# Gate and up products with the tokens stationary and 512 weight columns moving

## The chip, the cores and the metric

One core of a Trainium2 chip runs the whole program. The metric is the device time of one execution in microseconds (us). Before the change the median of 3 runs is 1294.36 us (1293.99 to 1295.44).

In what follows TensorE (PE) multiplies matrices: a *stationary* 128x128 operand is loaded first (PEld), then the columns of a *moving* operand stream through it and the result adds up in a PSUM bank of 128x512 float32. VectorE (DVE), ScalarE (ACT) and GpSimd (POOL) do the elementwise work, SyncE's queue (SP) issues the loads.

## The reference

One decoder layer on 256 tokens of width 2048: four recurrent mixers, an output product, and then the part that the change touches:

```
n = rmsnorm(x, ffn_norm)                                   # x: 256 x 2048
x = x + (silu(n @ w_gate) * (n @ w_up)) @ w_down           # w_gate, w_up: 2048 x 5632, w_down: 5632 x 2048
return rmsnorm(x, final_norm)
```

All inputs and the output are float32.

## The kernel before

**Products in three parts.** A float32 operand is split into a high part (rounded to the float32r format) and a low part (the rest). A product is high x high + high x low + low x high, that is three matmuls: the helper `mm3` (lines 167 to 172) issues them from lines 169, 170 and 171.

**Weights.** All weights lie in DRAM as blocks of 128 x 1024 float32 (512 KB) in the order of use, listed by `plan` (lines 45 to 55). `weights` (line 149) traces the load of a block on SP's queue (`raw`, 4 buffers), the rounding on ACT (`whi`, 3 buffers) and the subtraction on DVE (`wlo`, 3 buffers); it traces them with a raised priority (`PRIO` = 20), so that a planner, which orders each engine's instructions by priority and readiness, puts them ahead of about 20 instructions traced before them.

**Stages.** The mixers run first, between products with `w_in`. Then `w_out` (line 1183) adds the output product to x, and by `transpose_in` (line 361) transposes the new x on TensorE: two k tiles go through one bank, ACT writes the high part into `nhi[128, 16, 256]` (hidden position on the partitions, k tile, token), DVE the low part into `nlo`. The last four k tiles are made by `first()` inside the first gate product.

**Gate and up before (`ffn`, line 1240, with `group`, line 374).** 22 steps, each with 256 hidden channels of gate and 256 of up. A block of weights is 4 k tiles x 256 columns, so a product takes 4 blocks. The weights are the stationary side (128 channels), the 256 tokens of `nhi` or `nlo` the moving side:

```
a = (bank[:, h * T : h * T + T], w[0][:, kk, hs], w[1][:, kk, hs], *acts[k])
```

This is 16 k tiles x 2 channel halves x 3 = 96 matmuls of 256 columns per product, 4224 in all. The result lies with channels on the partitions, so the scale of a token (`rs1`, one number per token) must lie along the free dimension: `scales` (line 262) spreads it to a tile `R` with two small float32 matmuls. DVE multiplies the gate bank by `R` (line 1254), ACT takes the silu (line 1255), DVE multiplies the up bank by `R` (line 1256), and POOL multiplies both (line 1257) into the tiles `H`, which already have the layout that the down product needs.

**Down (`ffn`, lines 1273 to 1304).** Two passes over 44 k tiles with 1024 output columns each. Here `H`, split by `split` (line 1175), is the stationary side (128 tokens), and 512 weight columns are the moving side: 12 matmuls of 512 columns per block, 1056 in all, in four banks per pass. Between the passes DVE adds the four banks to x (`add`, line 1265). After the second pass come the last norm and the output.

**Banks.** After the mixers `bank` (line 115) hands out the 8 PSUM banks in a fixed rotation of their three pools (`big` with 3, `mx` with 4, `mxl` with 1 bank).

Of the kernel before, what the change touches and what calls it, by code (L numbers as in the profile page):

```python
# [9 lines left out]
AF = mybir.ActivationFunctionType  # L10
ALU = mybir.AluOpType
PSUM = bass.MemoryType.PSUM
P = 128
# [29 lines left out]


def plan():
    """the 128 x 1024 blocks that the weights are loaded in: (array, first row tile, row tiles, first column, columns)"""
    units = []
    cols = [RW + c for c in range(0, 1792, 256)] + [RG + c for c in range(0, 1024, 256)] + [o + c for o in (GD, ML) for c in range(0, 2048, 256)]
    for c in cols:
        units += [("w_in", k, 4, c, 256) for k in range(0, KT, 4)]  # L50
    units += [("w_out", k, 2, c, 512) for c in range(0, D, 512) for k in range(0, KT, 2)]
    for c in range(0, HID, 256):
        units += [(w, k, 4, c, 256) for w in ("ffn_w_gate", "ffn_w_up") for k in range(0, KT, 4)]
    units += [("ffn_w_down", k, 1, c, 1024) for c in range(0, D, 1024) for k in range(HT)]
    return units

# [2 lines left out]


def lay_out(inputs):
    """the inputs in the layouts that the kernel loads; nothing but reshapes, transposes, slices and concatenations"""
    import numpy as np

    A = {k: np.asarray(v) if k == "final_norm" else np.asarray(v)[0] for k, v in inputs.items()}
    r = {"x": A["x"], "final_norm": A["final_norm"]}
    r["xT"] = A["x"].T.reshape(KT, P, T).transpose(1, 0, 2)
    r["chan"] = np.concatenate([A[k].reshape(n, P) for k, n in CHAN]).T
    u = np.empty((len(UNIT_AT), P, UNIT), A["w_in"].dtype)
    for (w, k, nk, c, n), i in UNIT_AT.items():  # L70
        u[i] = A[w][k * P : (k + nk) * P, c : c + n].reshape(nk, P, n).transpose(1, 0, 2).reshape(P, UNIT)
    r["units"] = u
    g = np.concatenate([A["w_in"][:, o + 2048 : o + 2056] for o in (GD, ML)], axis=1)
    r["gate_w"] = g.reshape(KT, P, 16).transpose(1, 0, 2).reshape(P, 256)
    z = np.zeros(4, g.dtype)
    r["gate_b"] = np.stack([np.concatenate([A["gdn_dt_bias"], z, A["mlstm_b_i"], A["mlstm_b_f"]]), np.concatenate([A["gdn_a_log"], z, z, z])], axis=1)
    r["lora"] = np.concatenate([np.concatenate([A["rwkv_w2"], A["rwkv_a2"]]), A["rwkv_g2"]], axis=1)
    r["rglru"] = np.concatenate([A[k].transpose(1, 0, 2).reshape(P, 512) for k in ("rglru_w_a", "rglru_w_x")], axis=1)
    return {k: np.ascontiguousarray(v) for k, v in r.items()}


class Emitter:
# [30 lines left out]
        return self.pp.tile([P, 512], F32, name=self.nm("mxl"), tag="mxl", bufs=1)  # L113

    def bank(self):
        """a PSUM bank for the large products: from all of them once the mixers are done"""
        if self.gens or self.phase == 1:
            return self.big()
        self.nb += 1
        return (self.big, self.mx, self.big, self.mx, self.big, self.mx, self.mxl, self.mx)[self.nb % 8]()  # L120
# [4 lines left out]
        self.slot_of = {}  # L125

    def S(self, k=1, c="A"):
        """a [128, 512 k] tile in the rotating slots of lifetime class c"""
        key = c if k == 1 else "D"
        if not self.free_slots[key]:  # L130
            keys = [x for x in ("A", "B", "L", "D") if self.free_slots[x] and (k == 1 or x == "D")]
            if not keys:
                raise MemoryError(f"no slot for {key}")
            key = keys[0]
        q = self.free_slots[key]
        i = q.pop(0)
        w = 1024 if key == "D" else 512
        t = self.spool.tile([P, w], F32, name=self.nm(f"s{key}{i}"), tag=f"slot{key}{i}")
        if w != 512 * k:
            t = t[:, 0 : 512 * k]  # L140
        self.slot_of[id(t)] = (key, i, t)
        return t
# [29 lines left out]
        return i  # L172

    def behind(self):
        """PE instructions of the block stay behind the large products traced so far"""
        return self.tc.issue_after(self.last_mm.ins)

    def tick(self, k=1):
        """the mixers' next steps; HOLD has the ticks by which a step is late, to let its operands come"""
        self.acc += k  # L180
        while self.acc >= 1:
            self.acc -= 1
            for g in list(self.gens):
                name, gen, step, hold = g
                if hold:
                    g[3] -= 1
                    continue
                try:
                    next(gen)
                except StopIteration:  # L190
                    self.gens.remove(g)
                g[2] += 1
                g[3] = HOLD.get((name, g[2]), 0)
# [55 lines left out]
        return banks  # L249

    def squares(self, c):
        """sums of squares of x's columns 512c..512c+511; the last call gives the reciprocal roots"""
        nc = self.nc
        xs = self.S(2)
        nc.sync.dma_start(xs.rearrange("p (a n) -> p a n", a=2), self.A["x"].rearrange("(a p) d -> p a d", p=P)[:, :, c * 512 : c * 512 + 512])
        nc.scalar.activation(xs[:, 0:512], xs[:, 0:512], AF.Square, accum_out=self.ss[:, 0, c : c + 1])
        nc.vector.scalar_tensor_tensor(xs[:, 512:1024], xs[:, 512:1024], 1.0, xs[:, 512:1024], op0=ALU.mult, op1=ALU.mult, accum_out=self.ss[:, 1, c : c + 1])
        self.free(xs)
        if c == 3:
            self.rs0 = self.rstd(self.ss, "rs0")  # L260

    def scales(self, rs):
        """R: rs[token] on every partition"""
        nc = self.nc
        z = self.mx()
        for a in range(2):
# [13 lines left out]
        return i  # L280

    def normalise(self, u):
        """the normalised activations of k tiles 2u and 2u + 1, from the unnormalised parts"""
        nc = self.nc
        hi, lo = self.nhi[:, 2 * u : 2 * u + 2, :], self.nlo[:, 2 * u : 2 * u + 2, :]
        f = self.xt[u // 2].rearrange("p (k t) -> p k t", k=4)[:, 2 * (u % 2) : 2 * (u % 2) + 2, :]
# [85 lines left out]
                nc.vector.scalar_tensor_tensor(self.nlo[:, k, :], t[:, j * T : j * T + T], wcol[:, k : k + 1], self.nhi[:, k, :].bitcast(F32), op0=ALU.mult, op1=ALU.subtract)  # L372

    def group(self, name, col, tm=False, acts=None, pre=None):
        """products with 256 columns of a weight: two halves of a bank, by channel tile or (tm) by token tile"""
        bank = self.bank()
        acts = acts or [(self.nhi[:, k, :], self.nlo[:, k, :]) for k in range(KT)]
        first = None
# [20 lines left out]


class Lag:
    """TensorE instructions of the mixers, ordered behind the next few large products"""

    def __init__(self, em):
        self.em = em
# [8 lines left out]


def sums(em, mat, t, wait=0):
    """mat' t for a matrix of few bits, t in two parts"""
    nc = em.nc
    hi, lo = em.S(c="B"), em.S(c="B")
    h, l = hi.bitcast(F32R), lo.bitcast(F32R)  # L420
# [24 lines left out]


def evict(f):
    """the instructions that empty a bank of the large products go before those of the mixers"""

    def g(em, *a, **k):  # L450
        with em.tc.high_priority(offset=EPRIO):
# [36 lines left out]


def solve_blocks(em, q0, nq, steps, n=32):  # L490
    """inv <- (I - M)^-1 per partition; blk holds M transposed ([q, tau, t]), inv starts as the identity"""
    nc = em.nc
    blk, inv, tmp = em.blk[q0 : q0 + nq], em.inv[q0 : q0 + nq], em.tmp[q0 : q0 + nq]
    for j in range(n - 1):
# [24 lines left out]
def rwkv_half(em, hf, LX, R, K, V):  # L519
# [69 lines left out]
    sc = em.const([P, 2, 4], em.nm("sc"))  # L589
    nc.vector.tensor_tensor(sc[:, :, 0:3], E1.rearrange("p (a c t) -> p a c t", a=2, t=64)[:, :, 0:3, 63], em_.rearrange("p (a c) -> p a c", a=2)[:, :, 1:4], op=ALU.mult)  # L590
    em.free(E1, E2, E3, kk, a)
    # bonus
    for j in range(2):
        nc.vector.scalar_tensor_tensor(halves(t1)[j], halves(R)[j], PT["rwkv_r_k"][:, pr[j] : pr[j] + 1], halves(K)[j], op0=ALU.mult, op1=ALU.mult)
    em.free(R, K)
# [31 lines left out]
    def gmv(c, h, s):  # L627
        return GM[c // 2][:, (c % 2) * 512 + h * P + s * 64 : (c % 2) * 512 + h * P + s * 64 + 64]

    # token-major v and k,b  # L630
    VS, KT_ = em.S(2), em.S(2)
    nc.gpsimd.memset(VS[64:128, :], 0.0)
    for cc in range(2):
# [42 lines left out]
    nc.vector.tensor_copy(XT.rearrange("p (u n) -> p u n", n=64)[64:96, :, 32:64], zx[64:96, :].rearrange("p (u n) -> p u n", n=32))  # L676
    em.free(U)
    yield
    # chunk chain
    zy = em.mxl()  # L680
    sy = Seq(em)
    Y = None
# [83 lines left out]

@evict
def silu2(em, X, src=None):
    """X <- 2 silu(src)"""
    nc = em.nc  # L770
    src = X if src is None else src
    th = em.S()
# [20 lines left out]
def gates_mm(em):  # L793
# [41 lines left out]
    nc.scalar.activation(em.neg, GT[:, 1, 1, 0:4], AF.Exp, scale=-1.0)  # L835
    nc.vector.tensor_scalar(em.neg, em.neg, -1.0, None, op0=ALU.mult)
    yield
    # mLSTM: c = i - b, M = max(0, cummax c), exp(-m)
    em.c = em.const([P, 2, 4], "ccol")
    nc.vector.tensor_tensor(em.c, GT[:, 0, :, 8:12], GT[:, 1, :, 12:16], op=ALU.add)  # L840
    t = em.mx()
# [18 lines left out]


def bcast_rows(em, d, hf):
    """the rows 2hf and 2hf + 1 of d, on every partition"""
    z = em.S(c="B")
    em.nc.sync.dma_start(z, d[2 * hf : 2 * hf + 2].rearrange("h t -> (h t)").partition_broadcast(P))
    return z
# [292 lines left out]

@evict  # L1160
def gelu2(em, bank):
    """2 gelu(bank), tanh form; only needs the bank"""
    nc = em.nc
    g, t = em.S(), em.S()
    nc.scalar.activation(g, bank, AF.Copy, scale=0.5)
# [74 lines left out]
def ffn(em, first):  # L1240
    nc, A = em.nc, em.A
    H = []
    v2 = lambda t: t.rearrange("p (a b) -> p a b", a=2)
    for f in range(HID // 256):
        if f % 2 == 0:
            H.append(em.S(2))
        h = H[-1][:, (f % 2) * 512 : (f % 2) * 512 + 512]
        gb = em.group("ffn_w_gate", f * 256, pre=(lambda u: first() if u == 1 else None) if f == 0 else None)
        if f == 0:
            em.scales(em.rs1)  # L1250
        Rb = em.R[:, 0:T].unsqueeze(1).to_broadcast([P, 2, T])
        ub = em.group("ffn_w_up", f * 256)
        t, u = em.S(), em.S()
        nc.vector.tensor_tensor(v2(t), v2(gb), Rb, op=ALU.mult)
        nc.scalar.activation(t, t, AF.Silu)
        nc.vector.tensor_tensor(v2(u), v2(ub), Rb, op=ALU.mult)  # L1256
        nc.gpsimd.tensor_tensor(h, t, u, op=ALU.mult)  # L1257
        em.free(t, u)
    em.free(em.R)
    fn = [em.S() for _ in range(4)]  # L1260
    for n in range(4):
        nc.gpsimd.dma_start(fn[n], A["final_norm"][n * 512 : n * 512 + 512].partition_broadcast(P))
# [10 lines left out]
    for n in range(2):  # L1273
# [8 lines left out]
        for k in range(HT):  # L1282
            if k % 2 == 0:
                if hs and k <= HT - TAIL:
                    em.free(*hs)
                hs = split(em, H[k // 4][:, (k % 4) * T : (k % 4) * T + 512])
            whi, wlo = em.weights("ffn_w_down", k, 1, n * 1024, 1024)
            hi, lo = (t.bitcast(F32R) for t in hs)
            tail.append((k, hi, lo, whi, wlo))
            if n == 0 or k < HT - TAIL:  # L1290
# [146 lines left out]
```

## Time and profile before

| | |
|---|---|
| median of 3 runs | 1294.36 us |
| span of the profiled execution, first to last instruction | 1292.7 us |
| median less span | 1.66 us |
| PE busy | 97% of the span |
| DVE, ACT, POOL busy | 63%, 48%, 11% |
| granted TensorE clock, mean of the span | 0.991 |

The profile is of one execution and gives no time of it but the span; what lies before the first and after the last instruction is taken as the difference to the median. A line of the profile names engine, source line and operation, then `output<-input` by the program's names (`sA`, `sD` are the rotating SBUF slots, `big`, `mx`, `mxl` PSUM banks). Matmuls overlap, and a matmul's shown duration runs from its start to its modelled end. So what one of them costs in a stream is the distance from its start to the start of the next, not its duration.

### The profile page before, as it was taken

How to read it: one execution, taken by the hardware profiler on the slowest of the kernel's cores; microseconds unless marked ns; L12 is line 12 of the kernel's file. 1: busy time of each engine (PE TensorE's matmuls, PEld its weight loads, DVE VectorE, ACT ScalarE, POOL GpSimd, SP SyncE). 2: the span in 40 equal slices, each digit the busy share in tenths (PEclk: the TensorE clock that was granted, in tenths of full speed). 3: DMA queues.
4: the chain of work that ended last, by engine and by line, in shares of the span. 5: the costliest groups of instructions: out<-in, count | busy, mean ns of one | idle time of the engine just before them, and what ended most of it. 6: DMA issues, size and time to landing. Idle time of an engine off the chain costs nothing.

```text
span 1292.7 us, 22536 instructions
## 1 busy us (share of the span) xinstructions
PE 1259.0 (97%) x9244; PEld 1173.2 (91%) x9244; DVE 817.7 (63%) x1068; ACT 620.2 (48%) x809; POOL 142.4 (11%) x145
## 2 busy tenths in 40 slices
PE   9899999999899999999999999999999999999997
PEld 8789989988888888999999999999999988888885
DVE  6975799665698765755555555555555555557554
ACT  7664784436543544643333334333344444445443
POOL 1520210213401120000000000000100000001000
PEclk9999999999899999999999999999999999999999
DMA  8554436344544455555555555555655655555553
GB/s 328 184 161 125 139 117 184 129 151 131 166 160 134 136 170 194 171 183 183 180 180 185 189 181 180 180 191 185 201 194 177 193 184 194 195 195 188 191 193 127
DMA packets 72216, 227.25 MB, mean 176 GB/s; under 512 B 15752, under 2 KB 16016, under 8 KB 72112
## 3 DMA queue, kind: packets, MB, share of 16 engines
q1 hardware_dynamic: 71504, 224.14, 52.9%
q0 software_dynamic: 464, 1.57, 0.4%
q8 instruction: 72, 1.18, 0.4%
q14 instruction: 32, 0.26, 0.1%
q10 hardware_dynamic: 144, 0.10, 0.0%
HBM read 222.49 MB, written 3.28 MB: 175 GB/s over the span
## 4 chain that ended last, share of the span: by engine, by line
PE 85%; DVE 9%; issue 2%; ACT 1%; DMA 1%; POOL 1%; DVEq 0%; POOLq 0%; ACTq 0%; SPq 0%
PE big L171 13%; PE big L170 13%; PE big L169 13%; PE mx L170 10%; PE mx L171 10%; PE mx L169 10%; PE mx L409 4%; DVE wlo L274 3%; PE mxl L169 3%; PE mxl L170 3%; PE mxl L171 3%; PE big L277 2%; DVE sD L499 1%; DVE sD L500 1%; DVE sA L763 1%
## 5 line engine op out<-in xcount | busy, mean ns | idle before, releaser
L274 DVE TENSOR_TENSOR wlo<-raw,whi 128x1024 fp32r<-128x1024 f32 x396 | 510.1, 1289 | 326.9 <-ACT whi L274 325.6
L274 ACT ACTIVATE whi<-raw 128x1024 fp32r<-128x1024 f32 x396 | 418.4, 1057 | 491.8 <-PE mx L170 148.8
L171 PE MATMUL big<-nhi,wlo 128*128 128x256 f32 x1056 | 303.3, 287 | 3.4 <-DVE wlo L274 3.4
L170 PE MATMUL big<-nlo,whi 128*128 128x256 f32 x1056 | 303.7, 288 | 0.0
L169 PE MATMUL big<-nhi,whi 128*128 128x256 f32 x1056 | 302.9, 287 | 0.0
L171 PEld LDWEIGHTS big<-nhi,wlo 128*128 128x128 f32 x1056 | 203.9, 193 | 5.8 <-DVE wlo L274 4.2
L170 PEld LDWEIGHTS big<-nlo,whi 128*128 128x128 f32 x1056 | 203.8, 193 | 2.3 <-issue 1.1
L169 PEld LDWEIGHTS big<-nhi,whi 128*128 128x128 f32 x1056 | 203.8, 193 | 1.9 <-issue 0.7
L169 PE MATMUL mx<-nhi,whi 128*128 128x256 f32 x704 | 199.4, 283 | 0.0
L170 PE MATMUL mx<-nlo,whi 128*128 128x256 f32 x704 | 199.2, 283 | 0.0
L171 PE MATMUL mx<-nhi,wlo 128*128 128x256 f32 x704 | 199.2, 283 | 0.0
L170 PEld LDWEIGHTS mx<-nlo,whi 128*128 128x128 f32 x704 | 135.2, 192 | 0.0
L169 PEld LDWEIGHTS mx<-nhi,whi 128*128 128x128 f32 x704 | 135.1, 192 | 0.0
L171 PEld LDWEIGHTS mx<-nhi,wlo 128*128 128x128 f32 x704 | 135.1, 192 | 0.0
L169 PE MATMUL big<-whi,sA 128*128 128x512 f32 x216 | 84.9, 393 | 0.0
L170 PE MATMUL big<-wlo,sA 128*128 128x512 f32 x216 | 84.6, 392 | 0.0
L170 PE MATMUL mx<-wlo,sA 128*128 128x512 f32 x216 | 84.3, 390 | 0.1
L169 PE MATMUL mx<-whi,sA 128*128 128x512 f32 x216 | 84.3, 390 | 0.0
L171 PE MATMUL mx<-whi,sA 128*128 128x512 f32 x212 | 82.5, 389 | 0.0
L1257 POOL TENSOR_TENSOR sD<-sA,sA 128x512 f32<-128x512 f32 x22 | 29.2, 1327 | 474.5 <-DVE sA L1256 409.9
L171 PE MATMUL big<-whi,sA 128*128 128x512 f32 x204 | 79.4, 391 | 1.7 <-DVE sA L1179 1.7
L170 PE MATMUL big<-wlo,nhi 128*128 128x256 f32 x192 | 56.5, 294 | 3.8 <-DVE wlo L274 3.8
(400 smaller groups left out, 1866.2 us busy)
## 6 DMA issues: line engine op xcount, KB each, us to landing
raw<-in_units SPq DMA_DIRECT2D x404, 512.0 KB, 3.5
sD<-in_x SPq DMA_DIRECT2D x8, 512.0 KB, 4.6
sD<-in_xT SPq DMA_DIRECT2D x4, 512.0 KB, 6.0
out_y<-sD SPq DMA_DIRECT2D x8, 256.0 KB, 2.9
sA<-in_final_norm POOLq DMA_DIRECT2D x4, 256.0 KB, 4.3
sD<-in_lora SPq DMA_DIRECT2D x1, 512.0 KB, 7.0
sD<-in_rglru POOLq DMA_DIRECT2D x1, 512.0 KB, 3.9
dr<-sD SPq DMA_DIRECT2D x2, 256.0 KB, 3.8
```

The source lines that it names most:

```text
L169: i = nc.tensor.matmul(out, ahi, bhi, start=start, stop=False, skip_group_check=True)
L170: nc.tensor.matmul(out, ahi, blo, start=False, stop=False, skip_group_check=True)
L171: self.last_mm = nc.tensor.matmul(out, alo, bhi, start=False, stop=stop, skip_group_check=True)
L274: i = fn(*a, **k)
L277: i = fn(*a, **k)
L409: return self.em.nc.tensor.matmul(*a, **k)
L499: nc.vector.tensor_tensor(tv, col, row, op=ALU.mult)
L500: nc.vector.tensor_tensor(inv[:, j + 1 : n, 0:b], inv[:, j + 1 : n, 0:b], tv, op=ALU.add)
L763: nc.vector.scalar_tensor_tensor(o[:, d:T], u[:, 0 : T - d], tap[3 - d], o[:, d:T], op0=ALU.mult, op1=ALU.add)
L1257: nc.gpsimd.tensor_tensor(h, t, u, op=ALU.mult)
```

## The change

Gate and up are computed in 11 steps of 512 hidden channels. A block of weights is now 2 k tiles x 512 columns (8 blocks per product, as many blocks as before in all). The stationary side is a 128-token slice of `nhi` or `nlo`, the moving side 512 weight columns, and each product fills two banks, one per half of the tokens: 8 blocks x 2 halves x 2 k tiles x 3 = 96 matmuls of 512 columns per product, 2112 in all. Tokens are on the partitions now, so the scale of a token is one number per partition: ACT takes the silu of the gate bank with `rs1` as its scale, and one DVE instruction per bank multiplies the up bank by `rs1` and by the silu. `scales`, the tile `R` and POOL's products go. The result `h` has tokens on the partitions and must be transposed for the down product: `turn` issues 8 transposes of 128x128 float32 on TensorE into two banks, and ACT copies the banks into `H`. The transposes of a step are traced in the next step's gate product after the weights of its third block, those of the last step in the down product's first pass after the weights of k tile 2.

```diff
@@ def plan():
-    for c in range(0, HID, 256):
-        units += [(w, k, 4, c, 256) for w in ("ffn_w_gate", "ffn_w_up") for k in range(0, KT, 4)]
+    for c in range(0, HID, 512):
+        units += [(w, k, 2, c, 512) for w in ("ffn_w_gate", "ffn_w_up") for k in range(0, KT, 2)]
...
@@ def ffn(em, first):
-    v2 = lambda t: t.rearrange("p (a b) -> p a b", a=2)
-    for f in range(HID // 256):
-        if f % 2 == 0:
-            H.append(em.S(2))
-        h = H[-1][:, (f % 2) * 512 : (f % 2) * 512 + 512]
-        gb = em.group("ffn_w_gate", f * 256, pre=(lambda u: first() if u == 1 else None) if f == 0 else None)
-        if f == 0:
-            em.scales(em.rs1)
-        Rb = em.R[:, 0:T].unsqueeze(1).to_broadcast([P, 2, T])
-        ub = em.group("ffn_w_up", f * 256)
-        t, u = em.S(), em.S()
-        nc.vector.tensor_tensor(v2(t), v2(gb), Rb, op=ALU.mult)
-        nc.scalar.activation(t, t, AF.Silu)
-        nc.vector.tensor_tensor(v2(u), v2(ub), Rb, op=ALU.mult)
-        nc.gpsimd.tensor_tensor(h, t, u, op=ALU.mult)
-        em.free(t, u)
-    em.free(em.R)
+    late = None
+
+    def group(name, col, pre):
+
+        banks = [em.bank(), em.bank()]
+        for u in range(KT // 2):
+            w = em.weights(name, 2 * u, 2, col, 512)
+            pre(u)
+            for a in range(2):
+                ts = slice(a * P, a * P + P)
+                for kk in range(2):
+                    k = 2 * u + kk
+                    em.mm3(banks[a], em.nhi[:, k, ts], em.nlo[:, k, ts], w[0][:, kk, :], w[1][:, kk, :], start=k == 0, stop=k == KT - 1)
+        return banks
+
+    def turn(h):
+
+        H.append(em.S(2))
+        for i in range(2):
+            z = em.bank()
+            for j in range(2):
+                for a in range(2):
+                    nc.tensor.transpose(z[:, j * T + a * P : j * T + a * P + P], h[a][:, (2 * i + j) * P : (2 * i + j) * P + P], em.ident)
+            nc.scalar.activation(H[-1][:, i * 512 : i * 512 + 512], z, AF.Copy)
+        em.free(*h)
+
+    for f in range(HID // 512):
+
+        def pre(u):
+            if f == 0 and u == 1:
+                first()
+            if late and u == 2:
+                turn(late)
+
+        gb = group("ffn_w_gate", f * 512, pre)
+        t = [em.S(), em.S()]
+        for a in range(2):
+            nc.scalar.activation(t[a], gb[a], AF.Silu, scale=em.rs1[:, a : a + 1])
+        ub = group("ffn_w_up", f * 512, lambda u: None)
+        for a in range(2):
+            nc.vector.scalar_tensor_tensor(t[a], ub[a], em.rs1[:, a : a + 1], t[a], op0=ALU.mult, op1=ALU.mult)
+        late = t
...
             whi, wlo = em.weights("ffn_w_down", k, 1, n * 1024, 1024)
+            if n == 0 and k == 2:
+                turn(late)
             hi, lo = (t.bitcast(F32R) for t in hs)
```

## Rows read from the trace of the kernel before

**Rows 1.** Page, head and part 1: busy time (share of span) and instructions.
```profile
span 1292.7 us, 22536 instructions
PE 1259.0 (97%) x9244; PEld 1173.2 (91%) x9244; DVE 817.7 (63%) x1068; ACT 620.2 (48%) x809; POOL 142.4 (11%) x145
```
**Rows 2.** Page, part 4: the chain that ended last, by engine.
```profile
PE 85%; DVE 9%; issue 2%; ACT 1%; DMA 1%; POOL 1%; DVEq 0%; POOLq 0%; ACTq 0%; SPq 0%
```
**Rows 3.** Stages: stretch, length, busy PE, PEld, DVE, ACT, POOL; clock, DMA share, GB/s.
```profile
535.29:1043.53 508.24, 508.24 (x4239) 508.24 (x4237) 272.31 (x234) 205.21 (x215) 30.95 (x26) 1.00 0.57 185
1043.53:1163.24 119.71, 119.71 (x531) 99.11 (x529) 69.83 (x67) 57.79 (x66) 1.61 (x2) 1.00 0.59 194
```
**Rows 4.** Timeline of PE, gate/up: start, duration, instruction; 44 starts apart.
```profile
899.89 0.28 PE L169 MATMUL big<-nhi,whi 128*128 128x256 f32 x1
...
905.17 0.28 PE L171 MATMUL big<-nhi,wlo 128*128 128x256 f32 x1
```
**Rows 5.** Timeline of PE, down, first pass: 48 starts apart.
```profile
1149.64 0.39 PE L169 MATMUL mx<-whi,sA 128*128 128x512 f32 x1
...
1160.52 0.39 PE L169 MATMUL mx<-whi,sA 128*128 128x512 f32 x1
```
**Rows 6.** Timeline of PE where down begins.
```profile
1043.53 0.40 PE L169 MATMUL mx<-whi,sA 128*128 128x512 f32 x1
...
1044.00 0.39 PE L171 MATMUL mx<-whi,sA 128*128 128x512 f32 x1
```
**Rows 7.** Timeline of PE around eight transposes (L368) between 512-column matmuls.
```profile
521.58 0.39 PE L171 MATMUL big<-whi,sA 128*128 128x512 f32 x1
521.81 0.60 PE L368 MATMUL mx<-ident,sD 128*128 128x128 f32 x4
...
522.60 0.48 PE L169 MATMUL mx<-whi,sA 128*128 128x512 f32 x1
522.91 0.39 PE L170 MATMUL mx<-wlo,sA 128*128 128x512 f32 x1
```
**Rows 8.** Line 368: durations in ns (min/median/max), first and last start.
```profile
L368 PE MATMUL mx<-ident,sD x16: 270/273/273, 521.8 to 539.0; 128*128 128x128 f32 x16
```
**Rows 9.** Timeline of PE around the matmuls of `scales` (L267).
```profile
547.62 0.28 PE L171 MATMUL mx<-nhi,wlo 128*128 128x256 f32 x1
547.74 0.60 PE L267 MATMUL mx<-ident,rs 128*128 128x128 f32 x4
...
548.30 0.28 PE L170 MATMUL mxl<-nlo,whi 128*128 128x256 f32 x1
```
**Rows 10.** Groups by line, gate/up: count, busy us, mean ns, idle before, releasers.
```profile
L274 DVE TENSOR_TENSOR wlo<-raw,whi 128x1024 fp32r<-128x1024 f32 x176 | 236.6, 1344 | 204.6 <-ACT whi L274 204.4
L274 ACT ACTIVATE whi<-raw 128x1024 fp32r<-128x1024 f32 x176 | 186.4, 1059 | 296.4 <-PE mx L170 148.8 <-PE big L170 84.8 <-PE mxl L170 30.7
L1255 ACT ACTIVATE sA<-sA 128x512 f32<-128x512 f32 x22 | 13.6, 616 | 0.6 <-DVE sA L1254 0.6
L1256 DVE TENSOR_TENSOR sA<-big,sA 128x512 f32<-128x512 f32 x15 | 10.4, 692 | 11.0 <-PE big L171 11.0
L372 DVE SCALAR_TENSOR_TENSOR nlo<-big,chan,nhi 128x256 fp32r<-128x256 f32 x4 | 1.9, 478 | 0.2 <-ACT nhi L371 0.2
L371 ACT ACTIVATE nhi<-big,chan 128x256 fp32r<-128x256 f32 x4 | 1.9, 468 | 1.0 <-DVE nlo L372 1.0
```
**Rows 11.** Page, part 6: loads of weight blocks, KB each, us to landing.
```profile
raw<-in_units SPq DMA_DIRECT2D x404, 512.0 KB, 3.5
```
**Rows 12.** Timeline of DVE at the end of down's first pass: two of four adds.
```profile
1161.40 0.69 DVE L274 TENSOR_TENSOR sD<-sD,mx 128x512 f32<-128x512 f32 x1 [1.08 <-PE mx L171]
...
1163.14 0.68 DVE L274 TENSOR_TENSOR sD<-sD,big 128x512 f32<-128x512 f32 x1
```
**Rows 13.** Timeline of PE, down's second pass: first matmuls into its banks.
```profile
1163.24 0.39 PE L169 MATMUL mx<-whi,sA 128*128 128x512 f32 x1
...
1165.28 0.39 PE L169 MATMUL big<-whi,sA 128*128 128x512 f32 x1
```

## The prediction

> **What bounds the kernel now.** I read the head of the page first: PE is busy for 97% of the span and no other engine for more than 63% [rows 1], and the chain that ended last lies on PE for 85% [rows 2]. Such shares are means over unlike stages, so the second view is the table by stage. From the start of gate/up to the start of down, 508.24 us, PE is busy for all 508.24 us at clock 1.00, with DVE at 272 us and ACT at 205 us; down's first pass is the same picture over 119.71 us [rows 3]. So what the change is worth is decided by how many TensorE instructions there are and at what pace they follow each other. Busy time can't show the pace, as the shown durations overlap; the third view, the timeline of PE, can. In gate/up 44 matmuls of 256 columns start within 5.28 us, one per 0.1200 us [rows 4], though each is shown with 0.28 us. In down 48 matmuls of 512 columns start within 10.88 us, one per 0.2267 us [rows 5]. Check: 4224 x 0.1200 = 506.9 us, and the eight transposes and the four matmuls priced below (0.88 and 0.44 us) make it 508.2 of the 508.24 us [rows 3]; 528 x 0.2267 = 119.7 of 119.71. Both stages are streams of matmuls without a hole. Twice 0.1200 is 0.2400, so a matmul costs 13.3 ns beside its columns, and half as many of twice the width save that once per pair.
>
> **The change part by part.** All sums are made against the profiled execution, span 1292.7 us [rows 1]; the median is 1.66 us above it, and I add that at the end.
>
> *Gate and up matmuls.* Removed: 4224 x 0.1200 = 506.88 us. Added: 2112 x 0.2267 = 478.72 us. Result -28.16 us, all on the path. The shape of the new matmul (128 tokens stationary, 512 float32r weight columns moving) is that of down, so its pace is read from a row and not inferred from the width. Bounds: the 13.3 ns could vanish from the saving (0.2400 per matmul: no gain), and the slowest pace in rows is 0.235 us, the first three matmuls of down [rows 6]; the stage as a whole averages 119.71 / 528 = 0.2267 [rows 3], so I take 0.2267.
>
> The Trainium skill ("TensorE: Matmul & The Clock Gate", Back-to-back issue gap) gives a rule that speaks against this edit: a warm matmul follows the one before after its columns at 2.4 GHz plus about 2.5 ns. By it two of 256 columns would cost 218.3 ns and one of 512 215.8, the edit would save 2112 x 2.5 ns = 5.3 us, less than the transposes cost. The trace disagrees: it has 120.0 and 226.7 ns [rows 4, 5], a fixed part five times as large, and I go by the trace.
>
> *Transposes.* 11 steps x 8. Eight of them stand between 512-column matmuls in the stage before: from the start of the last matmul ahead of them (521.58) to the start of the second one behind them (522.91) are 1.33 us, of which two matmuls take 0.45, so 0.88 us for eight, about 0.11 each, with the slower first matmul behind them counted in [rows 7]. 11 x 0.88 = +9.64 us, on the path, as TensorE has no hole to take them. The upper bound is the shown duration, 0.273 us each [rows 8], if they followed one another without overlap: 24.0 us. They overlap in the trace (four are shown as 0.60 us, not 1.09), so I take 0.88. The Trainium skill (same page, Part 4: PE-mode transpose) states about 275 ns for a transpose in a kernel; as a price per transpose that would be 24.2 us. The duration in the trace agrees with it, the distance between starts (0.11 us) doesn't.
>
> *`scales`.* Its four small matmuls go: 548.30 - 547.62 = 0.68 us, less two matmuls of 0.12, so -0.44 us [rows 9]. The next late thing would be `rs1` itself; before, line 267 reads it at 547.74 [rows 9], 12.5 us into the stage that starts at 535.29 [rows 3], and the first silu now comes after eight blocks, 8 x 2.72 = 21.8 us.
>
> *ACT, DVE, POOL.* Per step (192 matmuls and eight transposes, 44.4 us) ACT has 16 `whi` of 1.06 us, two silus and two copies of 0.62 us; read from PSUM they may cost up to 0.94 each, twice the 256-element 0.468 [rows 10]. That is 19.4 to 20.7 us of 44.4. DVE has 16 `wlo` of up to 1.34 us and two products of 0.69 to 0.96 (twice 0.478) [rows 10], 23 us of 44.4; before, it had four of 0.69 for the same 512 channels. POOL's products go altogether. None of this bounds: cost 0, covered by PE; without that cover it would be at most the two copies, 1.2 to 1.9 us per step.
>
> *The new wait on PE.* The transposes wait for `h`, and every later matmul is queued behind them. They stand behind two whole blocks of the next gate product, so PE reaches them 24 x 0.2267 = 5.44 us after the last up matmul. `h` needs at worst a `wlo` that has just begun (1.34) and both products (1.92): 3.3 us. Margin 2.1 us, so the wait costs 0. If the planner issued the transposes one block sooner, 3.3 - 2.72 = 0.6 us per step would show.
>
> *The new wait on ACT.* The copies out of the transposes' banks wait for PE, and the next `whi` is queued behind them. ACT is ahead: its idle time before `whi` ends with PE's release of a buffer (nearly all of 296 us) [rows 10], which means that it fills each of the three buffers as soon as it is free, two blocks before use. A delay of up to a block (2.72 us) stays unseen, and the eight transposes take 0.88. Cost 0.
>
> *Banks.* A step takes six banks of a rotation of eight, so each comes back a step or more after its last reader began, with one exception: the extra pair for the last transposes shifts the rotation in down, and by my count the single `mxl` bank then serves both the second bank of the first pass and the last of the second. It must be emptied before the tenth matmul of the second pass, 2.04 us in [rows 13]; before, the corresponding add ends at 1163.14 + 0.68 = 1163.82 [rows 12], 1.46 us ahead of that place. Cost 0, at most about 1 us if the adds get one `wlo` later.
>
> *Loads.* As many blocks of the same 512 KB, on SP's queue in the same order of use, each now needed every 2.72 instead of 2.88 us. A load lands 3.5 us after issue and four buffers are in rotation [rows 11]; down takes them at this very pace, 194 GB/s against 185, with PE never idle [rows 3]. Cost 0. The down product's own splits of `H` only need tiles that were turned several steps before.
>
> Sum: -28.16 + 9.64 - 0.44 = -18.96 us. Span 1273.7 us, and with 1.66 us around it **1275.4 us**.
>
> **The rivals.**
>
> *A. PE waits for `h` (or a bank) at each step.* For it: the wait is new and serial with everything behind it. Against: the margin of 2.1 us, and that DVE has over 40% of its time idle in this stage [rows 3]. With the transposes a block sooner, 11 x 0.6 = 6.6 us: 1282 us.
>
> *B. The transposes cost their durations.* For it: 0.273 us shown each [rows 8]. Against: eight in 0.88 us [rows 7]. 24.0 instead of 9.64 us: 1289.8 us.
>
> *C. Slower: a 512-column matmul with `nhi` stationary keeps no fixed part to save.* Place: each of the 2112 matmuls. The change turns slower where the pace passes 0.2400 - (9.64 - 0.44) / 2112 = 0.2356 us; at 0.2400 the time is 1294.4 + 9.2 = 1303.6 us. For it: the first matmuls of down at 0.235 [rows 6], which everywhere would give 1293. Against: the mean of a whole pass, 0.2267 [rows 3]. By the rule of the Trainium skill cited above 5.3 us would be saved on the way, and the time would be 1298.3 us; no 512-column stream in this trace runs so.
>
> *D. The prefetch falls behind.* 512 KB per 2.72 us is what down does without a wait [rows 3]; a miss of 0.1 us per block, on 176 blocks, would be 17.6 us and leave 1293.
>
> **How the numbers follow.** The forecast holds with 0.86, and its own range is 1274 (every matmul at 0.226) to 1278 (0.2 us of waiting per step). A: 0.07. B: 0.02. C: 0.03, of which 0.02 beyond the bound for slower. D: 0.02. For 8 in 10 I take 1273 to 1280: the forecast's range, a little below it for stalls that may go, and the smaller half of A. A change of 0.2% (2.6 us) is about what a measurement of this kernel can tell from none; so faster 0.95 (forecast, A and B), within 0.03 (D and the nearer part of C), slower 0.02.
>
> **What would show it.** Gate/up matmuls with 512 columns every 0.227 us, at clock 1.00; groups of eight transposes followed by a matmul 0.88 us later than without them; no idle time of PE that ends with DVE's product or ACT's copy; gate/up (with ten of the eleven groups) some 488 us long instead of 508; down as long as before plus 0.88. The prediction is wrong if the pace in gate/up exceeds 0.229, if eight transposes hold TensorE for more than 1.2 us, or if PE waits at the start of a step.

## The result and the profile after

The changed kernel takes 1277.74 us (median of 4 runs, 1275.4 to 1281.97) against 1294.17 us of the kernel before, run beside it; the ratio is 0.9872, 95% interval 0.9848 to 0.9897. The forecast of 1275.4 us is a ratio of 0.9855, inside the interval. The profiled execution is the run of 1275.4 us; its span is 1273.4 us, forecast 1273.7.

The head and part 1 of the page after:

```profile
span 1273.4 us, 18370 instructions
PE 1241.5 (98%) x7216; PEld 1072.9 (84%) x7216; DVE 780.7 (61%) x1045; ACT 633.6 (50%) x831; POOL 112.3 (9%) x123
```

The table by stage after (stretch, length, busy PE, PEld, DVE, ACT, POOL with counts, clock, DMA share, GB/s); the stretches are all ahead of gate/up, gate/up, down's first pass, and its second up to the tail:

```profile
0.00:534.35 534.35, 511.72 (x3953) 468.60 (x3953) 399.58 (x691) 295.32 (x449) 101.60 (x112) 0.98 0.52 164
534.35:1023.18 488.83, 488.83 (x2203) 405.66 (x2201) 235.75 (x212) 217.27 (x235) 2.97 (x5) 1.00 0.64 192
1023.18:1143.79 120.61, 120.61 (x537) 99.93 (x536) 68.84 (x67) 58.66 (x68) 0.31 (x1) 1.00 0.64 192
1143.79:1255.76 111.97, 111.83 (x494) 92.27 (x493) 69.17 (x65) 55.81 (x68) 6.29 (x4) 1.00 0.61 184
```

Against [rows 3], gate/up went from 508.24 to 488.83 us, still with PE busy all through at clock 1.00, and down's first pass from 119.71 to 120.61, 0.90 more, with the last group of transposes in it. Down's second pass takes 111.97 us where it took 111.96. So the gain is fewer instructions at the same fullness, not less waiting: from the start of gate/up to the tail the view of PE's waits lists none, before and after. PEld (the loads of the stationary operand), which was busy for all of gate/up, now has gaps: half as many loads.

The pace, from the timeline of PE in gate/up after (start, duration, instruction); the two rows are 48 starts apart, 10.88 us, so 0.2267 us per matmul, the pace of down in [rows 5]:

```profile
699.95 0.39 PE L169 MATMUL big<-whi,nhi 128*128 128x512 f32 x1
...
710.83 0.39 PE L169 MATMUL big<-whi,nhi 128*128 128x512 f32 x1
```

The seam between two steps, from the timeline of all engines after. Line 1283 is DVE's product that makes `h`, line 1265 the transposes, line 1266 ACT's copies:

```profile
578.60 0.74 DVE L1283 SCALAR_TENSOR_TENSOR sA<-mx,rs,sA 128x512 f32<-128x512 f32 x1
578.66 0.39 PE L171 MATMUL big<-whi,nlo 128*128 128x512 f32 x1
...
579.26 0.74 DVE L1283 SCALAR_TENSOR_TENSOR sA<-big,rs,sA 128x512 f32<-128x512 f32 x1
...
584.10 0.40 PE L171 MATMUL big<-whi,nlo 128*128 128x512 f32 x1
...
584.33 0.60 PE L1265 MATMUL mx<-ident,sA 128*128 128x128 f32 x4
...
584.77 0.60 PE L1265 MATMUL big<-ident,sA 128*128 128x128 f32 x4
585.12 0.47 PE L169 MATMUL mx<-whi,nhi 128*128 128x512 f32 x1
585.44 0.39 PE L170 MATMUL mx<-wlo,nhi 128*128 128x512 f32 x1
585.50 0.58 ACT L1266 ACTIVATE sD<-mx 128x512 f32<-128x512 f32 x1
...
587.05 0.40 PE L171 MATMUL big<-whi,nlo 128*128 128x512 f32 x1
```

The last up matmul starts at 578.66, `h` (the product that has to be transposed) is whole at 579.26 + 0.74 = 580.00, and the transposes start at 584.33, 4.3 us later: no wait. From 584.10 to 585.44 are 1.34 us, less two matmuls 0.89 us, where [rows 7] gave 0.88. The groups of ACT and DVE in gate/up after (count, busy us, mean ns, idle before, releasers), answering to [rows 10]:

```profile
L274 DVE TENSOR_TENSOR wlo<-raw,whi 128x1024 fp32r<-128x1024 f32 x176 | 215.7, 1226 | 251.8 <-ACT whi L274 251.8
L274 ACT ACTIVATE whi<-raw 128x1024 fp32r<-128x1024 f32 x176 | 186.6, 1060 | 260.7 <-PE big L171 200.0 <-PE mxl L171 60.7
L1283 DVE SCALAR_TENSOR_TENSOR sA<-mx,rs,sA 128x512 f32<-128x512 f32 x11 | 8.2, 744 | 0.0
L1280 ACT ACTIVATE sA<-mx,rs 128x512 f32<-128x512 f32 x11 | 7.6, 690 | 3.0 <-PE mx L171 3.0
L1266 ACT ACTIVATE sD<-mx 128x512 f32<-128x512 f32 x10 | 5.8, 582 | 0.0
```

`wlo` takes 1.226 us on average instead of 1.344. In the kernel before, it took long only where it ran beside POOL's product: 22 of the 176 took 2.18 us on average, the other 154 1.23. One of the 22, from the timelines of POOL and DVE before:

```profile
906.39 1.29 POOL L1257 TENSOR_TENSOR sD<-sA,sA 128x512 f32<-128x512 f32 x1 [21.75 <-DVE sA L1256]
906.46 2.30 DVE L274 TENSOR_TENSOR wlo<-raw,whi 128x1024 fp32r<-128x1024 f32 x1 [0.21 <-ACT whi L274]
```

POOL's products are gone, and none of the 176 now takes more than 1.226 us. ACT still waits for PE's release of a buffer before 163 of the 176 `whi`, so it has time to spare, and the copies delay nothing that PE sees.

### The profile page after: what moved, and what is told of

The parts are those of the page before. It is cut to its first block, busy times and chain, and to the rows that moved or that the text cites. A ratio compares the mean times of both kernels' runs of the same rounds, so it can differ in the third digit from the quotient of the medians.

```text
span 1273.4 us, 18370 instructions
## 1 busy us (share of the span) xinstructions
PE 1241.5 (98%) x7216; PEld 1072.9 (84%) x7216; DVE 780.7 (61%) x1045; ACT 633.6 (50%) x831; POOL 112.3 (9%) x123
## 4 chain that ended last, share of the span: by engine, by line
PE 85%; DVE 8%; issue 2%; ACT 2%; DMA 1%; POOL 1%; DVEq 0%; POOLq 0%; SPq 0%; ACTq 0%
PE big L171 13%; PE big L170 13%; PE big L169 13%; PE mx L170 10%; PE mx L171 10%; PE mx L169 10%; PE mx L409 4%; PE mxl L169 3%; PE mxl L171 3%; PE mxl L170 3%; DVE wlo L274 3%; PE big L277 2%; DVE sD L499 1%; DVE sD L500 1%; DVE sA L763 1%
## 5 line engine op out<-in xcount | busy, mean ns | idle before, releaser
L170 PE MATMUL big<-wlo,nhi 128*128 128x512 f32 (+1 forms) x464 | 163.3, 352 | 3.6 <-DVE wlo L274 3.6
L169 PE MATMUL big<-whi,nhi 128*128 128x512 f32 (+1 forms) x464 | 162.1, 349 | 0.7 <-ACT whi L274 0.7
L171 PE MATMUL big<-whi,nlo 128*128 128x512 f32 (+1 forms) x464 | 162.4, 350 | 0.0
L171 PE MATMUL big<-nhi,wlo 128*128 128x256 f32 x544 | 157.8, 290 | 3.6 <-DVE wlo L274 3.6
L170 PE MATMUL big<-nlo,whi 128*128 128x256 f32 x544 | 158.1, 291 | 0.0
L169 PE MATMUL big<-nhi,whi 128*128 128x256 f32 x544 | 157.6, 290 | 0.0
L169 PE MATMUL mx<-whi,nhi 128*128 128x512 f32 x352 | 138.0, 392 | 0.0
L171 PE MATMUL mx<-whi,nlo 128*128 128x512 f32 x352 | 137.0, 389 | 0.0
L170 PE MATMUL mx<-wlo,nhi 128*128 128x512 f32 x352 | 137.0, 389 | 0.0
L171 PEld LDWEIGHTS big<-nhi,wlo 128*128 128x128 f32 x544 | 104.9, 193 | 6.0 <-DVE wlo L274 4.4
L170 PEld LDWEIGHTS mx<-wlo,nhi 128*128 128x128 f32 x352 | 66.1, 188 | 13.3
```

Source lines behind the costliest of these rows:

```text
L169: i = nc.tensor.matmul(out, ahi, bhi, start=start, stop=False, skip_group_check=True)
L170: nc.tensor.matmul(out, ahi, blo, start=False, stop=False, skip_group_check=True)
L171: self.last_mm = nc.tensor.matmul(out, alo, bhi, start=False, stop=stop, skip_group_check=True)
```

## The experiments

All are variants of the changed kernel; their edits are shown shortened, with cuts marked by `...`. Since what lies ahead of gate/up varies from execution to execution by a few us (below), each is read first by its gate/up stage, which in the changed kernel is 488.83 us in both executions that were profiled.

**The transposes left out.**

```diff
-            z = em.bank()
-            for j in range(2):
-                for a in range(2):
-                    nc.tensor.transpose(z[...], h[a][...], em.ident)
-            nc.scalar.activation(H[-1][:, i * 512 : i * 512 + 512], z, AF.Copy)
+            nc.scalar.activation(H[-1][:, i * 512 : i * 512 + 512], h[i], AF.Copy)
```

> The changed kernel without its 88 transposes of h: ACT copies h from SBUF straight into H, untransposed (so this leaves out the transposition of h). Theory 1 (mine: eight transposes hold TensorE for 0.88 us and nothing hides them): 11 x 0.88 = 9.7 us less than the changed kernel, span 1273.4 - 9.7 = 1263.7, time about 1265.7; gate/up, from its first 512-column matmul to the first of down, 488.8 - 8.8 = 480.0 us. Rival (each costs its shown 0.272 us): 24 us less, span 1249. Rival (the transposes fill time in which TensorE would have waited anyway): no change, 1273.4.

Measured 1266.44 us (1265.5 to 1274.96), ratio 0.9793 (0.9758 to 0.9827). The stage, in the columns of the table above:

```profile
535.72:1015.45 479.73, 479.73 (x2123) 397.35 (x2121) 235.71 (x212) 217.95 (x235) 2.97 (x5) 1.00 0.66 195
```

479.73 against 480.0 expected. Ten groups of eight cost 488.83 - 479.73 = 9.10 us, 0.91 each. Both rivals fall: not 0.272 us per transpose, and nothing hides them.

**256 columns, tokens still stationary.**

```diff
-                    em.mm3(banks[a], em.nhi[:, k, ts], em.nlo[:, k, ts], w[0][:, kk, :], w[1][:, kk, :], start=k == 0, stop=k == KT - 1)
+                    for c in range(2):
+                        cs = slice(c * 256, c * 256 + 256)
+                        x = (banks[a][:, cs], em.nhi[:, k, ts], em.nlo[:, k, ts], w[0][:, kk, cs], w[1][:, kk, cs])
...
```

The lines left out issue the three matmuls on each half; in the first k tile the second half is ordered behind the first.

> The changed kernel with every 512-column matmul of gate and up split into two of 256 columns: tokens still stationary, transposes still there, 4224 matmuls. Theory 1 (a matmul costs its columns and 13.3 ns, whichever side the weights are on): pace 0.1200 us, gate/up 488.8 + 28.2 = 517.0 us, span 1301.6, time 1303.6, slower than the kernel before by the transposes alone. Rival (the pace hangs on the stationary side, tokens against weights): pace 0.1133, gate/up 488.8, span 1273.4.

Measured 1304.13 us, ratio 1.0071 (1.0052 to 1.0091). The stage, and two matmuls 45 starts apart (5.40 us, 0.1200 each):

```profile
534.85:1051.27 516.42, 516.42 (x4316) 516.42 (x4314) 235.84 (x212) 216.89 (x235) 2.96 (x5) 1.00 0.55 182
```
```profile
699.77 0.28 PE L170 MATMUL mx<-wlo,nhi 128*128 128x256 f32 x1
...
705.17 0.28 PE L170 MATMUL big<-wlo,nhi 128*128 128x256 f32 x1
```

The side is no cause: at 256 columns the pace is 0.1200 us with the weights stationary [rows 4] and with the tokens stationary. Turning the sides alone makes the kernel slower, by about what the transposes cost (1304.13 us against 1295.28 of the kernel before); the width saves the rest.

**128 columns.** The same edit with four pieces.

> The changed kernel with every 512-column matmul of gate and up split into four of 128 columns, 8448 matmuls. Theory 1 (13.3 ns per matmul beside its columns, also at 128): pace 53.3 + 13.3 = 66.7 ns, gate/up 488.8 - 478.7 + 563.2 = 573.3 us, span 1357.9, time 1360. Rival (the load of the stationary operand sets a floor that 256 columns just cover; 128-column transposes follow each other at 0.109 us): 8448 x 0.109 = 921 us, gate/up 931, span 1715. In between, a floor of 0.100 us would give span 1640.

Measured 1739.1 us, ratio 1.3431 (1.3409 to 1.3454). The stage, and two matmuls 48 starts apart (5.36 us, 0.1117 each):

```profile
534.25:1486.98 952.73, 952.73 (x8539) 952.73 (x8538) 238.04 (x212) 216.88 (x235) 2.96 (x5) 1.00 0.30 100
```
```profile
699.80 0.28 PE L169 MATMUL mxl<-whi,nhi 128*128 128x128 f32 x1
...
705.16 0.28 PE L169 MATMUL mxl<-whi,nhi 128*128 128x128 f32 x1
```

Theory 1 fails here. Its constant of 13.3 ns was worked out from the paces at 256 and 512 columns and had been tested at no third width; at 128, where it would add to a stream of 53.3 ns, a matmul holds TensorE for 0.1117 us. The rival's floor, 0.109 from the transposes, is nearly right (931 us expected, 953 measured). Whether the floor belongs to each matmul or to an average over several is what the next run asks; that the load of the stationary operand sets it, no run here isolates. The Trainium skill ("TensorE: Matmul & The Clock Gate", LDWEIGHTS) gives a load as its columns divided by 1.2, in ns. An estimate from that for 128 columns is 128 / 1.2 = 106.7 ns; the 111.7 ns of this row are near it.

**384 and 128 columns in turn.** As many loads as with two of 256, unequal streams:

```diff
+                    for c0, c1 in ((0, 384), (384, 512)):
...
+                    for i, (l, r) in enumerate(((0, 2), (0, 3), (1, 2))):
+                        for o, x in ((o0, x0), (o1, x1)):
...
+                                    last = mm(o, x[l], x[r], **kw)
```

The pairs (0, 2), (0, 3) and (1, 2) are the three parts; each is issued on 384 columns and then on 128.

> The changed kernel with every 512-column matmul of gate and up split into one of 384 and one of 128 columns, strictly in turn: 4224 matmuls, as many stationary loads as with two of 256. Since 128-column matmuls alone came every 0.112 us instead of 66.7 ns, two theories are left. Theory F1 (a matmul lasts its columns and 13.3 ns, but never less than the 0.112 us that its own stationary load takes): a pair 173.3 + 112 = 285 ns, gate/up 488.8 + 2112 x 0.0586 = 612.6 us, span 1397. Theory F2 (the load runs beside the matmul ahead, and only what is longer than that matmul shows): the load for the 128 columns hides behind 384, but the next load of 0.112 us, beside the 128 columns of 53.3 ns, doesn't: a pair 173.3 + 66.7 if it can run ahead two deep, 240 ns, gate/up 517.0, span 1301.5; if it can't, about 285 as in F1. So 517 speaks for an average over a queue of loads, 613 for a floor at each matmul.

Measured 1403.51 us, ratio 1.084 (1.0808 to 1.0871). The stage, and rows of PE's timeline. Line 1273 is the 384-column matmul that opens every third pair; from the first to the last of them shown are 33 pairs:

```profile
537.82:1152.38 614.56, 614.56 (x4315) 614.56 (x4314) 237.09 (x212) 217.02 (x235) 2.97 (x5) 1.00 0.44 153
```
```profile
700.29 0.39 PE L1273 MATMUL big<-whi,nhi 128*128 128x384 f32 x1
700.52 0.22 PE L1271 MATMUL big<-whi,nhi 128*128 128x128 f32 x1
700.58 0.45 PE L1271 MATMUL big<-wlo,nhi 128*128 128x384 f32 x2
...
701.15 0.39 PE L1273 MATMUL big<-whi,nhi 128*128 128x384 f32 x1
...
709.75 0.39 PE L1273 MATMUL mx<-whi,nhi 128*128 128x384 f32 x1
```

A pair takes (709.75 - 700.29) / 33 = 0.2867 us and the stage 614.6, near the sums of F1 (0.285 and 612.6). That excludes an average over a queue of loads (0.240 and 517). It does not show F1 itself: F2 gave the same 0.285 for a load that can't run two ahead, and within a pair the starts don't lie as F1 would have them, 0.23 us from the 384 columns to the 128 and 0.06 back, where F1 has 0.173 and 0.112. How the load and the two streams overlap inside a pair stays open.

**The transposes two blocks earlier.**

```diff
-            if late and u == 2:
+            if late and u == 0:
                 turn(late)
```

> The changed kernel with the transposes traced ahead of the first block's matmuls of the next gate product instead of the third's; in TensorE's order two of the eight stand right behind the last up matmul, three matmuls follow, then the other six. In the trace of the changed kernel the first matmul of the next step starts at 578.88 and the first half of h is done at 579.34, the second at 580.00. Theory 1 (the two blocks ahead are what hides the wait for h): the first pair waits 0.5 us and the second group nothing, and one more change between transposes and matmuls costs about 0.1: some 0.6 us in ten steps, span 1273.4 + 6 = 1279. By the bound of the prediction (3.3 us until h) it would be 33 us, span 1306. Rival (h comes in time anyway): span 1273.4 to 1274.4.

Measured 1281.14 us, ratio 0.9892 (0.9875 to 0.9909). The stage, and a seam between steps from the timeline of all engines:

```profile
534.68:1027.66 492.98, 490.86 (x2203) 404.27 (x2202) 235.76 (x212) 218.40 (x235) 2.96 (x5) 1.00 0.64 190
```
```profile
578.94 0.74 DVE L1283 SCALAR_TENSOR_TENSOR sA<-mx,rs,sA 128x512 f32<-128x512 f32 x1
579.00 0.39 PE L171 MATMUL big<-whi,nlo 128*128 128x512 f32 x1
...
579.74 0.33 PE L1265 MATMUL mx<-ident,sA 128*128 128x128 f32 x1 [0.35 <-DVE sA L1283]
```

The stage is 4.15 us longer (some 6 expected). The wait that PE shows here ends with DVE's product: 579.74 - 579.00 is 0.74 us where a matmul is followed after 0.23, so 0.5 us, as expected, but only in six of the ten steps, some 3 us of the 4.15. In the other four the planner let two matmuls of the next block go ahead of the first pair, and the distance is 0.28 or 0.29 us. So the two blocks are what hides the wait, and it is a small one: far from the 3.3 us per step that the prediction took as its worst case. Whether one block ahead would hide it as well was not run.

**The changed kernel again.**

> The changed kernel once more, as it is. Its first four runs were 1275.4, 1275.6, 1279.9 and 1282.0 us with a mean granted clock of 0.990, 0.993, 0.986 and 0.986. Theory 1 (the spread comes from stretches at the half clock in the mixers, ahead of the change): gate/up 488.8 us in the profile with the clock at 1.00 all through, whatever the run's time; runs between 1275 and 1282, the kernel before spread as well. Rival (the transposes let the clock fall in gate/up, in some executions): a stretch at 0.5 behind 534 us, and the kernel before without spread.

Measured 1277.17 us (1275.4 to 1278.27), ratio 0.9865 (0.985 to 0.9881); the kernel before, on the same chip, ran from 1292.53 to 1296.73 us. The stages ahead of gate/up, gate/up, and all behind it:

```profile
0.00:536.04 536.04, 510.35 (x3953) 467.51 (x3953) 400.52 (x691) 295.17 (x449) 101.50 (x112) 0.98 0.52 163
536.04:1024.87 488.83, 488.83 (x2203) 405.59 (x2201) 235.78 (x212) 217.27 (x235) 2.97 (x5) 1.00 0.63 192
1024.87:1275.00 250.13, 240.97 (x1065) 198.60 (x1063) 145.37 (x144) 120.98 (x148) 7.72 (x6) 0.99 0.60 183
```

Gate/up is the same to 0.01 us, at clock 1.00. The 1.7 us by which this span exceeds the first one lie ahead of it (536.04 against 534.35), where the mean granted clock is 0.98 in both. One stretch of the changed kernel's first profile, in the mixers, shows what lies behind such a mean: TensorE ran 16 matmuls in 4 us at a granted clock of 0.99 (all but at the upper level, 2.4 GHz), and in the next 3 us the clock was 0.50, the lower of its two levels (1.2 GHz):

```profile
115.00:119.00 4.00, 4.00 (x16) 2.12 (x15) 1.34 (x3) 1.99 (x5) 0.00 (x0) 0.99 0.51 192
119.00:122.00 3.00, 3.00 (x12) 2.62 (x11) 1.76 (x4) 1.16 (x3) 1.14 (x1) 0.50 0.01 3
```

Over the profiles of this study gate/up begins between 534.25 and 537.82 us, though the program ahead of it is the same. That fits theory 1. In no profile do the transposes let the clock fall: in gate/up it is 1.00 in the changed kernel and in every variant. The kernel without them spread even more, one of its four runs at 1274.96 us with a mean clock of 0.983, 8.4 us above the next. What made the two longest runs of the changed kernel (1279.9 and 1282.0 us) was not traced and stays open.

**The transposes off TensorE.** DVE transposes 32x32 blocks, DMAs on POOL's queue carry the blocks through DRAM to the right partitions:

```diff
-                    nc.tensor.transpose(z[...], h[a][...], em.ident)
-            nc.scalar.activation(H[-1][...], z, AF.Copy)
+        tv = tmp.rearrange("p (c j a t) -> p a j c t", c=4, j=4, a=2)
+        for a in range(2):
+            nc.vector.transpose(tv[:, a], h[a].rearrange("p (j c t) -> p j c t", j=4, c=4))
+        for g in range(4):
+            nc.gpsimd.dma_start(dr[:, :, g, :].rearrange("c i n -> i c n"), tmp[32 * g : 32 * g + 32].rearrange("p (c n) -> p c n", c=4))
+        nc.gpsimd.dma_start(H[-1], dr.rearrange("c i g n -> (c i) (g n)"))
...
-                hs = split(em, H[k // 4][:, (k % 4) * T : (k % 4) * T + 512])
+                hs = split_h(em, H[k // 4].rearrange("p (g x t) -> p x g t", g=4, x=8)[:, 2 * j : 2 * j + 4])
```

> The changed kernel with h transposed off TensorE: per step two DVE instructions transpose 32x32 blocks (128x512 each), four DMAs on POOL's queue write them to DRAM in rows of 1 KB, one reads them back as H with channels on the partitions; the split of H reads it in runs of 32 elements. No TensorE transposes of h, no ACT copies. Theory 1 (the transposes hold TensorE for 0.88 us per step and everything else has room): 9.7 us less than the changed kernel, span 1263.7, time 1265.7. Rival (11 x 1 MB more on the DMA engines in small packets, or POOL's issuing, delays the loads of weights or DVE's halves): TensorE waits for wlo or whi in gate/up, and the time lies between 1268 and 1285; from 0.88 us of waiting per step on nothing is gained, 1275.4.

Measured 1268.52 us (1266.44 to 1269.88) beside the 1277.17 of the changed kernel on the same chip, ratio to the kernel before 0.9797 (0.978 to 0.9813). The stage, and the new groups in it:

```profile
537.68:1017.42 479.74, 479.74 (x2123) 397.44 (x2122) 246.63 (x232) 208.01 (x215) 30.46 (x55) 1.00 0.70 217
```
```profile
L274 DVE TENSOR_TENSOR wlo<-raw,whi 128x1024 fp32r<-128x1024 f32 x176 | 215.3, 1223 | 232.5 <-ACT whi L274 232.5
L1274 POOL DMA_DIRECT2D dh<-sD x40 | 22.0, 556 | 295.1 <-DVE sD L1271 295.1
L1271 DVE STREAM_TRANSPOSE sD<-sA 128x512 f32<-128x512 f32 x20 | 14.0, 701 | 0.0
L1276 POOL DMA_DIRECT2D sD<-dh x10 | 5.6, 556 | 51.9 <-DMA dh<-sD 41.8 <-DMA raw<-in_units 10.1
```

The stage is that of the run without transposes (479.73) to 0.01 us: all of their cost is gone and nothing has come in its place, though the DMA engines now move 217 GB/s instead of 192. The DVE blocks take 0.70 us each, and `wlo` is as fast as in the changed kernel. The loads of the weight blocks, from part 6 of the two pages (the changed kernel, then this one; the last number is the median time from issue to landing):

```profile
raw<-in_units SPq DMA_DIRECT2D x404, 512.0 KB, 3.6
raw<-in_units SPq DMA_DIRECT2D x404, 512.0 KB, 3.8
```

The run without transposes, which has none of this traffic, has 3.8 as well, and PE waits for nothing in gate/up. All five runs of this version are faster than every run of the two kernels.

## Why the prediction was right

Point by point, by its own steps:

- *Matmuls* (-28.16 us). The pace was taken as 0.2267 us and is 0.2267. The stage with 256 columns is 516.42 - 488.83 = 27.59 us longer, the same term measured with the transposes in place, 0.57 us smaller than worked out.
- *Transposes* (+9.64). Ten groups measure 9.10 us, 0.91 each and not 0.88; the eleventh lies in down: all behind gate/up takes 249.35 us without it (1264.8 - 1015.45) and 250.2 or 250.13 with it, so 0.8 to 0.9. Together some 9.9. The price from the distance between starts was right, that from the shown durations (24 us) wrong.
- *`scales`* (-0.44; two matmuls in the source, four in the trace) went without a trace of its own: no run takes it alone. Without the transposes the stage is 508.24 - 479.73 = 28.51 us shorter than before, where this term and the matmuls give 28.60. With them it came out at -19.41 us, where the terms without the last group give -28.16 + 8.80 - 0.44 = -19.80.
- *The wait for `h`*. No wait, as forecast, but the margin was mis-sized: 4.3 us where 2.1 stood in the prediction, because that worst case put a whole `wlo` ahead of both products, while in the trace DVE makes the first product while TensorE is still on the second bank. It was no true bound either: the 1.34 us that it took as the longest `wlo` are the mean of the group [rows 10], and the longest before took 2.31. With POOL's products gone that did no harm. Rival A fell for this kernel and appeared, at 0.5 us in six of ten steps, as soon as the two blocks ahead were taken away.
- *ACT, DVE, banks, loads*. PE waited for none of them. The products took 0.74 us, the silus 0.69, the copies 0.58 to 0.59, all within their bounds or below. The bank that might have cost up to 1 us cost nothing: down's second pass is as long as before to 0.01 us.
- *Rival C*, a slower kernel from 0.2356 us per matmul on, is excluded by the pace. The rule of the Trainium skill ("TensorE: Matmul & The Clock Gate", Back-to-back issue gap) behind it, columns at 2.4 GHz plus about 2.5 ns, which that section gives for an isolated matmul and not for a stream of loads and matmuls, fails at every width run here: 0.1117 us at 128 columns, 0.1200 at 256, 0.2267 at 512, and 0.2867 for a pair of 384 and 128.
- *The median* is 2.3 us above the forecast, although the span is 0.3 below: the sum stands for one execution, and the runs of the two kernels scatter by 4.3 us (before, 1292.53 to 1296.87 over all comparisons) and 6.6 us (after). 1.7 us of that was traced, to the part ahead of gate/up; the rest was not. That the profiled run took the forecast 1275.4 us to the tenth is luck: it is the fastest of the four. The upper end of the forecast's own range (1278), which takes in the median, stood for waits of PE that did not come.

What the prediction had no proof of was why a 512-column matmul saves 13.3 ns. It read the pace off another stage with the same shape, and that alone carried it: two paces can't test a sum of two terms, and the constant it put behind them does not hold at 128 columns. What sets the pace at each width stays open.

## What to carry to other kernels

Price a stream of matmuls by the distance between starts in a stage that has the very shape, not by the shown duration and not by a formula. In this kernel a 256-column stream (0.1200 us) lies just above the 0.112 us that a matmul takes in a stream of 128 columns; 512 columns instead save 13.3 ns per matmul removed, and a layout change that has to be paid for on TensorE can eat a third of that (9.9 of 28 us). Where the bound engine has to transpose, look whether engines with idle time and the DMA queues can: here that gave the third back.

## What was not expected of the hardware

- 128-column matmuls came every 0.1117 us, and a 384/128 pair took 0.2867 us, more than two of 256 (0.2400) for the same columns and the same number of loads.
- The first matmuls behind a group of transposes follow each other more slowly than 0.2267 us: from 585.44 to 587.05 in the seam above the distance between starts is 0.230 us, seven times in a row. That accounts for some 0.02 us of the 0.03 by which a group costs more than 0.88.
- Writing and reading 1 MB per step through DRAM in 1 KB rows, some 25 GB/s more, kept no engine waiting that PE depends on: the stage is as long as without any transposition, 479.74 against 479.73 us.
- A `wlo` on DVE took 2.18 us on average where it ran beside POOL's product, and 1.23 elsewhere.
